# Moving the last wait of a ReLU-and-sum kernel from GpSimd to SyncE, and the semaphore clear to an earlier moment

## The chip, the cores and the metric

The kernel runs on one core of one Trainium2 chip. The metric is the device time of one execution in microseconds. Two numbers appear side by side throughout: the *time* of a run, and the *span* of the profile, which goes from the start of the program's first recorded instruction to the end of its last. The time is longer than the span (161.95 against 160.1 us in the first profile).

## The reference

```python
# x: (32, 512, 1024) float32
def reference(x):
    relu_x = np.maximum(x, 0)
    return np.sum(relu_x, axis=-1).astype(np.float32)   # (32, 512)
```

The kernel reads 67.11 MB and writes 0.07 MB.

## The kernel before

The 16384 rows are spread over 128 partitions, 128 rows each. SyncE issues all loads and all stores. ScalarE (ACT) clamps and VectorE (DVE) sums, or either one does both for a row. The last row of each partition comes in four pieces. Three stores write the sums out; the last one, 128 x 2 values, can only be issued when DVE has summed the last piece. A semaphore is used here as a counter that instructions raise and that other instructions wait for. Each load has one of its own, `act` and `dve` count finished instructions, and the three stores share `stored`.

What matters here is the end of the program. `relu_sum` ends with the third store, issued by SyncE:

```python
    # ... (relu_sum: loads, clamps, sums, two stores)
    nc.vector.tensor_scalar(                       # the last piece
        out=last[:, :], in0=last[:, :], scalar1=0.0, scalar2=None,
        op0=MAX, op1=ADD, accum_out=res[:, NT - 1 : NT],
    ).wait_op(sems.dve, before_last, "sem-ge").then_inc(sems.dve, 1)
    n_dve += 1
    store(NT - 2, 2, n_act, n_dve)                 # SyncE issues the last store
    return n_store
```

Then, in the closing block, GpSimd waits until all three stores have landed (16 increments each, 48 in the trace) and clears every semaphore of the kernel, with a drain and a range clear (one instruction for a range of semaphores: while it runs, from 159.93 to 160.06 us, the trace has one change of each of the kernel's 18, at 159.949 to 160.036) taken from the instructions that the framework had put there:

```python
    nc.cur_bb = nc.bb_map[tc.start_bb_name + "_end"]
    body = nc.cur_bb.bb.instructions
    clear = semaphore_clear(body)      # GpSimd: drain, range clear
    body.clear()
    nc.gpsimd.wait_ge(sems.stored, 16 * n_stores)
    body.extend(clear)
    # ...
```

GpSimd does nothing else in this kernel, apart from four memsets of 98 to 101 ns, a drain and three semaphore instructions, all over by 0.7 us.

## Time and profile before

| | before |
|---|---|
| time, median of the first 3 runs | 162.18 us (162.17 to 162.97) |
| profiled run: time / span | 161.95 / 160.1 us |
| DMA queue, share of 16 engines' span | 98.0% |
| DVE / ACT busy | 74% / 65% |
| last store, issue to landing | 1.4 us |

The first lines are from the page of the kernel before: the span, the busy times (engine, busy us, share, number of instructions) and the DMA queue (packets, MB, share).

```profile
span 160.1 us, 133 instructions
...
DVE 117.7 (74%) x43; ACT 104.2 (65%) x50; POOL 0.2 (0%) x4
...
q1 hardware_dynamic: 2592, 67.18, 98.0%
```

Its loads and stores keep the 16 DMA engines busy for 98.0% of the span, at 420 GB/s in the mean, so I take the kernel as bound by its loads almost from end to end. The change touches nothing of that, so the end has to be read closely. This is the instructions in order of time from 158.1 us on (start us, duration us, engine, line, operation):

```profile
157.92 0.43 DVE L205 TENSOR_SCALAR_CACHE_REDUCE piece<-piece 128x271 f32<-128x271 f32 x1
158.28 0.08 DVE L205 DVE_READ_ACCUMULATOR piece<-piece 128x1 f32 x1
158.39 0.33 SPq L105 DMA_DIRECT2D out_dram<-res  x1
```

That view leaves out drains and semaphore instructions, and so does the chain of waits, whose last line ends at 158.36 us:

```profile
157.92 0.44 DVE piece L205 x2
```

The chain says that the kernel's last work is DVE's. Yet the span lasts until 160.1. What fills the 1.7 us can be seen with the DMA issues (KB, us from issue to landing) and with the view of line 29 (`tc.close()`, where the framework made the instructions of the closing block; duration ns minimum/median/maximum, first and last start):

```profile
out_dram<-res SPq DMA_DIRECT2D x1, 1.0 KB, 1.4
```

```profile
engine op xcount: duration ns min/median/max, first and last start us, forms
L29 POOLq DRAIN  x1: 88/88/88, 159.8 to 159.8; - x1
L29 POOLq EVENT_SEMAPHORE_RANGE_CLEAR  x1: 136/136/136, 159.9 to 159.9; - x1
```

So the store takes 1.4 us, and GpSimd's drain and clear come after it. The trace splits the store's 1.39 us, from the start of the issue, into 0.82 us until its first packet starts (the issue itself lasts 0.33 us), 0.20 us of moving, and 0.37 us from the last packet's end to the last increment.

The views stop here, but the trace also records changes of semaphores, among them many that no instruction of the program names. Semaphore 2 is one of these. It moves in two groups at the end, and from 160.790 us on, ahead of the second group, 243 other semaphores change once each. I read the two groups as barriers, at which the engines wait for one another, and the changes between as a reset; the trace gives only the moments, so this is a reading. Read from the semaphore events, which no view of the profile prints (us from the span's start; the names of the engines are inferred, in the prediction and from the trace of the run s1_sync_clears below):

```
last increment of "stored" (the store has landed)   159.787
semaphore 2, first barrier:   1.003 PE   157.597 ACT   160.590 GpSimd   160.634 DVE   160.657 SyncE
                              then back  160.754  160.794  160.828  160.874
243 other semaphores change (the reset)             160.790 to 161.435
semaphore 2, second barrier                         161.704 to 162.061
```

By this reading each engine moves the semaphore once in the first barrier, one after the other: this is what *joining* the barrier means below. The four moves after the fifth are *the way back*. What follows the span, both barriers with the changes between them, is called the closing barriers below; the one that the engines join is the first.

The time of this run is 161.95 us, 0.11 us less than the last of these events.

### The profile page before, as it was taken

How to read it: one execution, taken by the hardware profiler on the slowest of the kernel's cores; microseconds unless marked ns; L12 is line 12 of the kernel's file. 1: busy time of each engine (PE TensorE's matmuls, PEld its weight loads, DVE VectorE, ACT ScalarE, POOL GpSimd, SP SyncE). 2: the span in 40 equal slices, each digit the busy share in tenths (PEclk: the TensorE clock that was granted, in tenths of full speed). 3: DMA queues.
4: the chain of work that ended last, by engine and by line, in shares of the span. 5: the costliest groups of instructions: out<-in, count | busy, mean ns of one | idle time of the engine just before them, and what ended most of it. 6: DMA issues, size and time to landing. Idle time of an engine off the chain costs nothing.

```text
span 160.1 us, 133 instructions
## 1 busy us (share of the span) xinstructions
DVE 117.7 (74%) x43; ACT 104.2 (65%) x50; POOL 0.2 (0%) x4
## 2 busy tenths in 40 slices
DVE  0000000009999499994999999999999999999994
ACT  3000059990799708995099942999239992599993
POOL 0000000000000000000000000000000000000000
DMA  7996996996996996997998999979969969999993
GB/s 262 524 524 262 524 524 262 524 524 262 524 508 278 524 508 278 524 475 311 524 409 377 524 393 393 524 328 459 524 278 508 524 262 524 393 393 422 409 400 96
DMA packets 2592, 67.18 MB, mean 420 GB/s; under 512 B 672, under 2 KB 1184, under 8 KB 1312
## 3 DMA queue, kind: packets, MB, share of 16 engines
q1 hardware_dynamic: 2592, 67.18, 98.0%
HBM read 67.11 MB, written 0.07 MB: 420 GB/s over the span
## 4 chain that ended last, share of the span: by engine, by line
DMA 43%; DVE 33%; ACT 17%; another core or an unknown queue 3%; SPq 1%; issue 0%
DVE res L120 32%; DMA io<-in_x_dram 25%; DMA piece<-in_x_dram 18%; ACT io L112 17%; SPq L94 1%; DVE piece L137 1%; DVE piece L205 0%
## 5 line engine op out<-in xcount | busy, mean ns | idle before, releaser
L120 DVE TENSOR_REDUCE res<-io 128x8 f32<-128x8192 f32 (+2 forms) x9 | 101.1, 11287 | 40.0 <-ACT io L112 40.0
L112 ACT ACTIVATE io<-io 128x8192 f32<-128x8192 f32 (+2 forms) x9 | 81.7, 9110 | 47.1 <-DMA io<-in_x_dram 47.1
L127 ACT ACTIVATE io<-io 128x1024 f32<-128x1024 f32 x20 | 20.9, 1043 | 5.4 <-DMA io<-in_x_dram 5.3
L137 DVE TENSOR_SCALAR_CACHE_REDUCE io<-io 128x1024 f32<-128x1024 f32 x13 | 15.0, 1214 | 0.2
L127 ACT ACTIVATION_READ_ACCUMULATOR io<-io 128x1 f32 x20 | 3.7, 187 | 0.0
L112 ACT ACT_TABLE_LOAD x1 | 1.3, 1283 | 0.8 <-PEq L259 0.8
L137 DVE TENSOR_SCALAR_CACHE_REDUCE piece<-piece 128x244 f32<-128x244 f32 (+2 forms) x3 | 1.2, 416 | 0.4 <-DMA piece<-in_x_dram 0.4
L137 DVE DVE_READ_ACCUMULATOR io<-io 128x1 f32 x13 | 1.1, 82 | 0.0
L205 DVE TENSOR_SCALAR_CACHE_REDUCE piece<-piece 128x271 f32<-128x271 f32 x1 | 0.4, 435 | 0.0
L137 DVE DVE_READ_ACCUMULATOR piece<-piece 128x1 f32 x3 | 0.3, 84 | 0.0
L259 POOL MEMSET const-bfloat16-1.0<- 128x1 bf16 x1 | 0.1, 101 | 0.0
L259 POOL MEMSET const-uint8-127<- 128x1 uint8 x1 | 0.1, 101 | 0.0
L259 POOL MEMSET const-float32-0.0<- 128x1 f32 x1 | 0.1, 98 | 0.2 <-issue 0.2
L259 POOL MEMSET const-float32-1.0<- 128x1 f32 x1 | 0.1, 98 | 0.0
L205 DVE DVE_READ_ACCUMULATOR piece<-piece 128x1 f32 x1 | 0.1, 82 | 0.0
## 6 DMA issues: line engine op xcount, KB each, us to landing
io<-in_x_dram SPq DMA_DIRECT2D x1, 4096.0 KB, 21.6
io<-in_x_dram SPq DMA_DIRECT2D x1, 2048.0 KB, 26.1
io<-in_x_dram SPq DMA_DIRECT2D x1, 1024.0 KB, 28.1
io<-in_x_dram SPq DMA_DIRECT2D x1, 512.0 KB, 28.9
piece<-in_x_dram SPq DMA_DIRECT2D x1, 134.0 KB, 28.5
piece<-in_x_dram SPq DMA_DIRECT2D x1, 130.0 KB, 28.6
piece<-in_x_dram SPq DMA_DIRECT2D x1, 126.0 KB, 28.7
piece<-in_x_dram SPq DMA_DIRECT2D x1, 122.0 KB, 28.8
```

What stands on the lines that cost most here:

```text
L94: dma = nc.sync.dma_start(out=dst, in_=src)
L112: i = nc.scalar.activation(out=ap, in_=ap, func=RELU)
L120: nc.vector.tensor_reduce(out=res[:, m : m + n], in_=ap, axis=mybir.AxisListType.X, op=ADD).wait_op(sems.act, n_act, "sem-ge").then_inc(se ...
L127: i = nc.scalar.activation(out=ap, in_=ap, func=RELU, accum_out=res[:, m : m + 1])
L137: i = nc.vector.tensor_scalar(out=ap, in0=ap, scalar1=0.0, scalar2=None, op0=MAX, op1=ADD, accum_out=accum_out,)
L205: nc.vector.tensor_scalar(out=last[:, :], in0=last[:, :], scalar1=0.0, scalar2=None, op0=MAX, op1=ADD, accum_out=res[:, NT - 1 : NT],).wai ...
L259: nc = _bacc.Bacc("TRN2", target_bir_lowering=False, num_devices=1)
```

## The change

The intent: GpSimd should not be the one to wait for the last store. SyncE waits for the stores and takes their semaphore down in the same instruction. GpSimd clears all other semaphores earlier, while the last store is under way; a new semaphore `issued`, raised by SyncE after the last issue, tells it when. The diff, without the removed helper `semaphore_clear`:

```diff
     nc.cur_bb = nc.bb_map[tc.start_bb_name + "_end"]
-    body = nc.cur_bb.bb.instructions
-    clear = semaphore_clear(body)
-    body.clear()
-    nc.gpsimd.wait_ge(sems.stored, 16 * n_stores)
-    body.extend(clear)
+    nc.cur_bb.bb.instructions.clear()
+    nc.sync.wait_ge(sems.stored, 16 * n_stores).then_inc(sems.stored, -16 * n_stores)
+    nums = sorted(s.num for s in (*sems.loads, sems.act, sems.dve, sems.issued))
+    cleared = range(nums[0], nums[-1] + 1)
+    assert len(cleared) == len(nums)
+    nc.gpsimd.wait_ge(sems.issued, 1)
+    nc.gpsimd.drain(semaphore_range=cleared)
+    nc.gpsimd.sem_clear(cleared)
...
         self.dve = tc.alloc_semaphore("dve")
+        self.issued = tc.alloc_semaphore("issued")
         self.stored = tc.alloc_semaphore("stored")
...
     store(NT - 2, 2, n_act, n_dve)
+    nc.sync.sem_inc(sems.issued, 1)
     return n_store
```

More of the change, by code (lines that the diff above doesn't have):

```diff
@@ L215, in relu_sum @@
     store(NT - 2, 2, n_act, n_dve)
+    nc.sync.sem_inc(sems.issued, 1)
     return n_store
-def semaphore_clear(instructions):
-    pool = [i for i in instructions if i.engine == mybir.EngineType.Pool]
-    at = next(
-        n for n, i in enumerate(pool) if getattr(i, "is_reset_sema", False)
-    )
-    return pool[at : at + 2]
 def issue_ahead_of_the_barrier(tc: tile.TileContext, n_loads: int):
```

## The prediction

> **What bounds the kernel now.** The busy line shows DMA near its limit almost everywhere (98.0% of the 16 engines' span, 420 GB/s mean); DVE is busy 74%, ACT 65%. The change touches none of that. It touches only what follows the last vector instruction, so I read that stage from the instructions in order of time and from the semaphore events of the trace:
>
> - 158.37 us: last DVE instruction ends. 158.39: SyncE issues the last store (0.33 us).
> - 159.79: the store's last semaphore increment arrives (1.4 us from issue to landing, DMA issues view).
> - 159.81: GpSimd's DRAIN passes its wait (88 ns); 159.93: the range clear (136 ns); it ends at 160.06, which ends the span of 160.1 us.
> - [...] semaphore 2 moves at 1.00, 157.60, 160.59, 160.63, 160.66 and then 160.75 to 160.87; [...] semaphore 2 moves again from 161.70 to 162.06.
>
> The moves at 1.00 and 157.60 follow the ends of PE's work and of ACT's (157.49, so 0.11 us later). DVE (done 158.37) and SyncE (done 158.73) left no own move before 160.59, so the engines join in a fixed order and the third one, which the others wait for, must be GpSimd. It joins 0.53 us after its clear ended. So the tail from landing to GpSimd's joining is 160.59 - 159.79 = 0.80 us, all on the critical path.
>
> **What the change does.** It adds one semaphore, one SyncE increment after the last store's issue, and one SyncE wait that also subtracts 48 (SyncE's semaphore instructions last 17 ns in this trace). It moves GpSimd's drain and clear to just after that increment: start about 158.76, end about 159.02, joining the barrier about 159.55 (my sums, from the same 0.25 and 0.53 us), some 0.24 us before the store lands. That work leaves the critical path. What stays is SyncE: wait passed at about 159.81, done 159.83, joining about 0.11 us later if it behaves as ACT did: 159.94 instead of the last join at 160.66. Estimated gain: 0.7 us[...]. The profile's span falls less, by 0.23 us to about 159.83, because 0.5 us of the gain lie after the last instruction.
>
> **Prediction: 161.50 us (range 161.25 to 161.95).** That is -0.4%. Chance of faster by over 2%: 0.01; within 2%: 0.98; slower by over 2%: 0.01.
>
> **What would show each step.** GpSimd's drain and clear start near 158.75 and end before 159.1, during the store. The last instruction is a SyncE semaphore instruction near 159.81. The third move of semaphore 2 comes near 159.55 and the last engine's join near 159.94; joining to end keeps its length (160.66 to 162.06, 1.40 us). Everything before 158.4 stays as it was; the store still takes 1.4 us.
>
> **What would make it wrong.** (1) The 0.53 us after GpSimd's clear may not be GpSimd's own: if any engine that leaves last pays it, SyncE pays it too and the gain is only about 0.25 us (161.9). (2) GpSimd's clear might take longer while transfers run, and join after SyncE. (3) One of three runs before took 162.97, 0.8 us above the others; noise in the loads of that size covers the gain. (4) The time may stop elsewhere than at the end of the closing barrier, so that less than all of the gain counts.

SyncE's join at 159.94 instead of 160.66 us is 0.72 us, put at 0.7 us, and the 162.18 us of before less 0.7 us is about 161.5 us. That a gain at the join reaches the end in full was an assumption of mine; in the traces the join comes 0.705 us earlier and the end 0.76 us.

## The result and the profile after

| | before | after |
|---|---|---|
| time, median of 6 runs | 162.13 us (161.98 to 162.97) | 161.31 us (161.06 to 161.45) |
| ratio | | 0.9941, 95% interval 0.9921 to 0.9961 |
| profiled run: time / span | 161.95 / 160.1 us | 161.37 / 160.0 us |
| last store, issue to landing | 1.4 us | 1.4 us |

Ratios are computed as the mean time of one kernel's fast runs over that of the other's of the same rounds, so they are not quite the ratio of the medians. In the later sets they are not quite the ratio of the plain means either; the gains given in us below are differences of plain means over all runs listed. Here the means are 162.24 and 161.29 us, a gain of 0.95 us, while the medians differ by 0.82 us. By the 2% mark the two kernels are the same; by the interval, the changed one is a little faster.

The same lines of the page of the changed kernel:

```profile
span 160.0 us, 135 instructions
...
DVE 117.7 (74%) x43; ACT 104.2 (65%) x50; POOL 0.2 (0%) x4
...
q1 hardware_dynamic: 2592, 67.18, 98.0%
```

Two instructions more, otherwise the same. The end in order of time, and the DMA issue of the last store:

```profile
158.11 0.43 DVE L209 TENSOR_SCALAR_CACHE_REDUCE piece<-piece 128x271 f32<-128x271 f32 x1
158.47 0.08 DVE L209 DVE_READ_ACCUMULATOR piece<-piece 128x1 f32 x1
158.58 0.33 SPq L109 DMA_DIRECT2D out_dram<-res  x1
```

```profile
out_dram<-res SPq DMA_DIRECT2D x1, 1.0 KB, 1.4
```

In this profiled run the last work came 0.19 us later than in the one of before, because the loads arrived later (the last increment for the third piece of the last row came at 157.429 us before and at 157.622 us here). Such shifts go both ways from run to run (the listed spans of before lie between 159.9 and 160.4 us); from here on the tail is therefore counted from the moment at which the store lands. The views of the lines that the change added (220: the increment; 45 and 46: drain and clear; 40: the last wait):

```profile
L220 SPq EVENT_SEMAPHORE  x1: 17/17/17, 159.0 to 159.0; - x1
...
L45 POOLq DRAIN  x1: 88/88/88, 159.0 to 159.0; - x1
...
L46 POOLq EVENT_SEMAPHORE_RANGE_CLEAR  x1: 136/136/136, 159.1 to 159.1; - x1
...
L40 SPq EVENT_SEMAPHORE  x1: 17/17/17, 160.0 to 160.0; - x1
```

The drain and the clear cost what they cost before, 88 and 136 ns, but they run at 159.0 and 159.1, ahead of the landing at 159.97. The SyncE wait is also to be seen among the waits of the DMA queue (engine and line, waited for, total us, times, longest us). It is put down to SyncE's own line, as the store that it waits for has no row of its own there:

```profile
SPq L40 <- SPq L40: 1.0, 1, 1.0
```

The semaphore events of both traces (the SyncE wait and GpSimd's drain and clear are instructions), in us after the store's landing:

```
                                           before    after
GpSimd: drain starts                       +0.024   -0.980
GpSimd: clear ends                         +0.277   -0.728
SyncE: last wait passes                       -     +0.017
semaphore 2: GpSimd joins                  +0.803   -0.201
             DVE joins                     +0.847   -0.157
             SyncE joins                   +0.870   +0.165
             next move (the way back)      +0.967   +0.210
             last move of first barrier    +1.087   +0.330
             last move of second barrier   +2.274   +1.513
```

The tail is 2.274 - 1.513 = 0.76 us shorter. Only 0.24 us of it lie inside the span (its end is 0.277 us after the landing before, 0.034 us after it now); 0.52 us lie after the span, in the closing barriers, which the page doesn't show. From the last move of the first barrier to the last of the second, both take 1.18 to 1.19 us.

### The profile page after: what moved, and what is told of

Same layout as the page of the kernel before. It is cut to its first block, busy times and chain, and to the rows that moved or that the text cites. A ratio compares the mean times of both kernels' runs of the same rounds, so it can differ in the third digit from the quotient of the medians.

```text
span 160.0 us, 135 instructions
## 1 busy us (share of the span) xinstructions
DVE 117.7 (74%) x43; ACT 104.2 (65%) x50; POOL 0.2 (0%) x4
## 4 chain that ended last, share of the span: by engine, by line
DMA 43%; DVE 33%; ACT 17%; another core or an unknown queue 3%; SPq 1%; issue 0%
DVE res L124 32%; DMA io<-in_x_dram 25%; DMA piece<-in_x_dram 18%; ACT io L116 17%; SPq L98 1%; DVE piece L141 1%; DVE piece L209 0%
```

## The experiments

Three sets, each on one chip with its own runs of the kernel before: first on chip 2, second on chip 1, third on chip 4. All gave correct results. Edits are shown against the changed kernel, unless said otherwise. The main question is where the 0.53 us between the end of GpSimd's clear and its joining come from, and whether the 0.95 us of the first rounds were all tail.

Two theories stood against each other for the first question: **G**, GpSimd needs this time to leave its program, whatever it did last; **C**, the range clear causes it, on any engine. For the second: **T**, only the tail changed; **R**, the work ahead of the last store became shorter as well.

### The kernel before against itself (n0_before_again)

No edit.

> The kernel before against itself, to see what five rounds can tell apart. Ratio 1.000, within 0.003 either way. In its trace the last store's landing to the last move of semaphore 2 takes 2.27 us, as in the first trace of before.

Measured: 162.04 us median against 161.91 us, ratio 1.0007 (0.9995 to 1.0020). Tail in the trace 2.276 us, against 2.274 in the first trace. Single runs range from 161.83 to 162.30, so differences of 0.2 us between two runs mean nothing, while the tail repeats within 0.003 us from trace to trace of one kernel (2.274 and 2.276 here, 1.513 to 1.516 in the changed kernel).

### The changed kernel again (a0_after_again, a1_after_third)

No edit.

> The changed kernel again. Theory T (only the tail after the landing changed): the landing to the last move of semaphore 2 takes 1.51 us, 0.76 us less than before, and the ratio is 0.9953; the 0.9941 of the first rounds was pulled down by one long run of before (162.97 us). Rival R (the change also shortens the work ahead of the store): the ratio is again 0.994 or less, and the store lands at least 0.15 us earlier after the span's start than in before, over several runs.

Measured: 161.26 against 161.91 us, ratio 0.9965 (0.9952 to 0.9979), a gain of 0.60 us in the mean; one of the five runs took 161.82, and the medians differ by 0.65 us. Tail 1.516 us. T's 0.9953 lies at the edge of the interval and R's 0.994 outside it. As that was no clear answer, it was run once more, on another chip:

> The changed kernel once more, on whatever chip this call gets. The tail in the traces is 0.76 us shorter than before, but the means of the first two comparisons differed by 0.95 and 0.60 us. If the difference is noise of the loads, this one falls between them, with the tail again at 1.51 us: ratio 0.9953, within 0.0015. If the first chip showed something of its own, this comes out near 0.9965 again.

Measured: 161.16 against 161.97 us, ratio 0.9949 (0.9936 to 0.9963), a gain of 0.82 us. Tail 1.514 us.

The three comparisons gave 0.95, 0.60 and 0.82 us, around the 0.76 us of the traces. R can be tested with the spans, since the span ends at a fixed distance after the landing (0.277 us before, 0.034 us after). Over the 32 runs of before whose spans are listed, the mean span is 160.12 us (spans are listed to 0.1 us), so the store lands at 159.84 on average; over the 16 runs of the changed kernel it is 159.93, so the store lands at 159.90. The changed kernel's stores land no earlier (0.06 us later, with runs scattering by 0.12 and 0.18 us, one standard deviation). R falls; T stands.

The number free of load noise is time less span: over the same runs it is 1.88 us before (1.84 to 1.93) and 1.35 us after (1.32 to 1.40). No run of one kernel overlaps with one of the other. That is the 0.5 us in the barrier; the other 0.24 us are the clear in the span.

### GpSimd waits last, but has nothing else to do then (g1_pool_last)

```diff
-    nc.sync.wait_ge(sems.stored, 16 * n_stores).then_inc(sems.stored, -16 * n_stores)
...
     nc.gpsimd.sem_clear(cleared)
+    nc.gpsimd.wait_ge(sems.stored, 16 * n_stores).then_inc(sems.stored, -16 * n_stores)
```

> GpSimd clears the others early, as in the changed kernel, but GpSimd itself, not SyncE, waits for the stores last and takes their semaphore down. Theory G (the 0.53 us that GpSimd takes to join the closing barrier belong to GpSimd, whatever it did last): it joins about 0.57 us after the landing, and the gain over before is about 0.24 us, ratio 0.9985. Theory C (the 0.53 us belong to the range clear): it joins about 0.15 us after the landing, two more hops follow, and the gain is about 0.70 us, ratio 0.9957.

Measured: 161.79 against 161.91 us, ratio 0.9991 (0.9977 to 1.0005). The view of its last wait:

```profile
L46 POOLq EVENT_SEMAPHORE  x1: 17/17/17, 159.8 to 159.8; - x1
```

Its last instruction is now a plain semaphore instruction of 17 ns, ending 0.041 us after the landing; it joins at 0.603 us, that is 0.56 us later. The tail is 2.071 us. G said 0.57 and C 0.15. The last instruction needn't be a clear for the delay: G stands for GpSimd. (GpSimd still cleared once, 0.76 us before its wait passed; a GpSimd that waits last and never clears was not run.) Most of the change's gain is gone, although the clear is as well hidden as in the changed kernel.

### SyncE does everything, GpSimd nothing (s1_sync_clears)

```diff
-    nc.sync.wait_ge(sems.stored, 16 * n_stores).then_inc(sems.stored, -16 * n_stores)
-    nums = sorted(s.num for s in (*sems.loads, sems.act, sems.dve, sems.issued))
+    nums = sorted(s.num for s in (*sems.loads, sems.act, sems.dve, sems.issued, sems.stored))
...
-    nc.gpsimd.wait_ge(sems.issued, 1)
-    nc.gpsimd.drain(semaphore_range=cleared)
-    nc.gpsimd.sem_clear(cleared)
+    nc.sync.wait_ge(sems.stored, 16 * n_stores)
+    nc.sync.drain(semaphore_range=cleared)
+    nc.sync.sem_clear(cleared)
...
-    nc.sync.sem_inc(sems.issued, 1)
```

> SyncE waits for the stores and then does the drain and the range clear of all semaphores itself; GpSimd has nothing to do at the end. Theory G: SyncE takes about 0.25 us for drain and clear and joins about 0.11 us after, 0.40 us after the landing; gain over before about 0.47 us, ratio 0.9971. Theory C: the 0.53 us go with the clear to SyncE; it joins about 0.80 us after the landing, gain under 0.12 us, ratio 0.9993 or more.

Measured: 161.42 against 161.91 us, ratio 0.9974 (0.9961 to 0.9987). The ratio is G's, but by two errors that cancelled. SyncE is quicker with the same two instructions than GpSimd: 7 ns for the drain, not 88, and for the clear 64 ns, not 136:

```profile
L44 SPq DRAIN  x1: 7/7/7, 159.9 to 159.9; - x1
...
L45 SPq EVENT_SEMAPHORE_RANGE_CLEAR  x1: 64/64/64, 159.9 to 159.9; - x1
```

The clear ends 0.133 us after the landing and SyncE joins at 0.244 us, 0.11 us later as G said and far from C's 0.80. The tail is 1.594 us, 0.68 us less than before, where I had expected 0.47. The time gained only 0.45 us in the mean, while the mean span was 160.2 us, with one run of 161.91: the last store landed late, by luck as far as five runs can tell. This trace also gives the order of the engines away: with GpSimd free, semaphore 2 moves at 157.673 (ACT), 157.711 (GpSimd), 158.579 (DVE, whose work ended at 158.434) and 160.099 (SyncE), each where that engine became free and not before its predecessor. A GpSimd that has had nothing to do joins 0.04 us after ACT.

### More work for GpSimd, to measure the slack (x2_more_clears, x8_more_clears)

```diff
-    nc.gpsimd.sem_clear(cleared)
+    for _ in range(3):          # 9 in the second kernel
+        nc.gpsimd.sem_clear(cleared)
```

> The changed kernel, with GpSimd's early range clear done three times instead of once. In the traces of the changed kernel GpSimd joins the closing barrier 0.20 us before the landing and SyncE 0.17 us after it; before, DVE's and SyncE's joins followed GpSimd's within 0.07 us. So I estimate a slack of about 0.30 us. Two more clears of 0.12 to 0.14 us move GpSimd's join by 0.24 to 0.28 us, to about 0.05 us after the landing. If GpSimd is off the critical path with that slack: SyncE's join and the last move stay at 0.17 and 1.51 us after the landing, ratio to before as the changed kernel's (0.9953). If GpSimd's work still counts: the last move comes 0.24 us or more later, ratio about 0.9968.

> The same with nine clears instead of one, eight more of 0.12 to 0.14 us: GpSimd would join 0.74 to 0.9 us after the landing and is on the critical path again. The last move of semaphore 2 comes 1.47 us after GpSimd's join (as before: 2.27 less 0.80), at 2.2 to 2.4 us after the landing; the whole gain is lost again, ratio to before 0.9996 to 1.0006. If it stays near 0.9953, GpSimd's join isn't what the closing barrier waits for and my reading of semaphore 2 is wrong.

Measured with three clears: 161.36 against 162.01 us, ratio 0.9958 (0.9946 to 0.9970). The clears last 132 to 136 ns but start every 0.16 us:

```profile
L47 POOLq EVENT_SEMAPHORE_RANGE_CLEAR  x3: 132/132/136, 159.0 to 159.4; - x3
```

So GpSimd joins at +0.110 us instead of the expected +0.05. The tail is 1.584 us, only 0.07 us longer than with one clear, though 0.31 us of work were added: the rest was slack. So neither outcome came true; the trace lies between them, and the ratio can't tell 0.9953 from 0.9968. As the last move comes 1.474 us after GpSimd's join (2.274 - 0.803 = 1.471 in the kernel before), GpSimd may join as late as +0.04 us before it counts, so the slack of the changed kernel is about 0.24 us, not the 0.30 that I had estimated.

Measured with nine: 162.25 against 162.01 us, ratio 1.0014 (1.0000 to 1.0027), one run of five at 162.89. (The plain means would give 1.0023; without that run they give 1.0015.)

```profile
L47 POOLq EVENT_SEMAPHORE_RANGE_CLEAR  x9: 132/132/136, 159.6 to 160.9; - x9
```

The last clear ends at +0.533 us, GpSimd joins at +1.061 (again 0.53 us later), and the tail is 2.534 us: the whole gain is lost and 0.26 us more, which is above the expected 2.2 to 2.4 us by the spacing of the clears; GpSimd's join and the ratio are above what was expected too. That the last move comes 1.02 us later than in the changed kernel (2.534 against 1.513 us), with GpSimd's join 1.26 us later, of which about 0.24 us were slack, shows that GpSimd's join is waited for, and supports the reading of semaphore 2.

### No clear at all (c0_no_clear)

```diff
-    nc.gpsimd.wait_ge(sems.issued, 1)
-    nc.gpsimd.drain(semaphore_range=cleared)
-    nc.gpsimd.sem_clear(cleared)
...
-    nc.sync.sem_inc(sems.issued, 1)
```

> The changed kernel without GpSimd's wait, drain and clear and without the semaphore that releases them; only SyncE's last wait with its subtraction is left. The other semaphores keep their counts[...]. If all of GpSimd's work was hidden: last move 1.51 us after the landing, ratio to before 0.9953, equal to the changed kernel. If the clear or SyncE's added increment cost something (for example by delaying the store's landing): issue to landing shorter than 1.39 us or last move earlier than 1.50 us.

Measured: 161.23 against 162.01 us, ratio 0.9955 (0.9943 to 0.9968). Issue to landing is 1.395 us (1.391 in the changed kernel), the tail 1.529 us (1.513). GpSimd's clear and SyncE's added increment cost nothing that the trace shows; hidden is hidden.

### ScalarE waits last (t1_scalar_last)

```diff
-    nc.sync.wait_ge(sems.stored, 16 * n_stores).then_inc(sems.stored, -16 * n_stores)
+    nc.scalar.wait_ge(sems.stored, 16 * n_stores).then_inc(sems.stored, -16 * n_stores)
```

> The changed kernel, with ScalarE instead of SyncE waiting for the stores last. ScalarE joins second, ahead of GpSimd, DVE and SyncE. If only GpSimd is slow to join: ScalarE joins about 0.15 us after the landing, three more hops of about 0.04 us follow, SyncE's join comes at 0.22 to 0.28 us, the last move at 1.6 us, about 0.1 us later than with SyncE, ratio to before 0.9958. If SyncE is special[...]: the last move at 2.0 us, ratio 0.9985.

Measured: 161.36 against 162.01 us, ratio 0.9963 (0.9951 to 0.9976). The wait is ACT's:

```profile
L40 ACTq EVENT_SEMAPHORE  x1: 17/17/17, 159.9 to 159.9; - x1
```

ACT joins at +0.183 us, 0.15 us after its wait ended; GpSimd, DVE and SyncE follow at +0.221, +0.264 and +0.288, and the way back starts at +0.385. The tail is 1.696 us, between before and after, 0.18 us longer than with SyncE where I had expected 0.1; had ACT needed GpSimd's 0.53 to 0.56 us, the rival outcome of 2.0 us would have come. So SyncE isn't special in being quick to join (ACT takes 0.15 us from the end of its wait, SyncE 0.13 us in the changed kernel); it has the best place of those measured, the last one in the order, so that no other engine has to follow.

### A drain for the last wait (d1_drain_waits)

```diff
-    nc.sync.wait_ge(sems.stored, 16 * n_stores).then_inc(sems.stored, -16 * n_stores)
+    nc.sync.wait_ge(sems.stored, 16 * n_stores)
+    nc.sync.drain()
...
-    nc.gpsimd.wait_ge(sems.issued, 1)
-    nc.gpsimd.drain(semaphore_range=cleared)
-    nc.gpsimd.sem_clear(cleared)
...
-    nc.sync.sem_inc(sems.issued, 1)
```

> A version meant to be a little better than the changed kernel: GpSimd has nothing to do at the end, and SyncE's last wait sits on a drain (7 ns in the trace where SyncE clears) instead of a semaphore instruction (17 ns); nothing is subtracted[...]. SyncE joins at about 0.02 + 0.01 + 0.11 = 0.14 us after the landing instead of 0.17, the last move at 1.48 us. In the time that is 0.03 us, too little to be told from the changed kernel: ratio to before 0.995. If the joining time doesn't depend on the instruction that waits: 0.17 and 1.51 us.

Measured: 161.19 against 161.97 us, ratio 0.9953 (0.9940 to 0.9965), beside the changed kernel's 161.16 us in the same rounds. SyncE joins at +0.145 us and the tail is 1.494 us, 0.02 us shorter than the changed kernel's, close to the 1.48 us hoped for; the time cannot show it. The kernel without a clear is the nearer comparison, as GpSimd is idle in both: against it the tail is 0.035 us shorter. It also leaves all counts of the kernel's semaphores in place at the end of the program; its runs gave correct results all the same. No version beats the changed kernel by anything measurable.

The tails together, from the landing of the last store, with the means of the runs beside them:

| kernel | last engine to finish | GpSimd joins | SyncE joins | tail | tail against before | mean time against before |
|---|---|---|---|---|---|---|
| before | GpSimd, clear | +0.803 | +0.870 | 2.274 | | |
| nine clears | GpSimd, clear | +1.061 | +1.127 | 2.534 | +0.26 | +0.37 |
| GpSimd waits last | GpSimd, wait | +0.603 | +0.670 | 2.071 | -0.20 | -0.19 |
| ScalarE waits last | ACT, wait | +0.221 | +0.288 | 1.696 | -0.58 | -0.58 |
| SyncE clears | SyncE, clear | early | +0.244 | 1.594 | -0.68 | -0.45 |
| three clears | GpSimd joins just late | +0.110 | +0.177 | 1.584 | -0.69 | -0.66 |
| no clear | SyncE, wait | early | +0.175 | 1.529 | -0.75 | -0.71 |
| changed kernel | SyncE, wait | -0.201 | +0.165 | 1.513 | -0.76 | -0.95, -0.60, -0.82 |
| drain waits | SyncE, drain | early | +0.145 | 1.494 | -0.78 | -0.75 |

"Early" means ahead of the last store's issue. The times follow the tails within 0.16 us, except in two comparisons that one long run pulled: the first of the changed kernel (0.19 us off, where a run of before took 162.97) and SyncE clears (0.23 us off). Without its run of 162.89 the nine clears' mean is 0.24 us above before, beside the 0.26 us of the tail.

## Why the prediction was right or wrong

**What bounds the kernel, and what the change touches: right.** The DMA queue is 98.0% busy before and after, and nothing ahead of the store changed that the runs can tell. Over the runs whose spans are listed the store lands at 159.84 us before and 159.90 us after.

**The tail as the only place of the gain: right.** GpSimd's drain and clear moved into the store's flight; the last instruction is SyncE's, 17 ns long, 0.017 us after the landing; GpSimd joins 0.20 us before the landing (I had said 0.24); SyncE joins at +0.165 us (I had said 0.15); the span falls by 0.24 us relative to the landing (I had said 0.23), and the larger part of the gain lies outside the span.

**The doubt about the 0.53 us: settled as the prediction had it.** They belong to GpSimd. It needs 0.53 to 0.56 us from its last instruction to joining, after a clear as after a plain wait, and whether a store is in flight or not (0.53 us before, with the changed kernel and with nine clears, 0.56 us in g1_pool_last); SyncE needs 0.11 to 0.14 us and ACT 0.11 to 0.15 us. What GpSimd does in this time is open: it executes no instruction of the program then, and no run here looks inside.

**The sum: too small by 0.06 us.** I predicted 0.7 us, and the traces show 0.76 us. SyncE's join came 0.705 us earlier (0.870 to 0.165), as foreseen. The term that failed is the stretch from SyncE's join to the last move, which I took as the same in both kernels ("joining to end keeps its length (160.66 to 162.06, 1.40 us)"). It shrank from 1.404 to 1.348 us. In all six traces in which DVE joins just ahead of SyncE, the way back starts 0.12 us after DVE's join (0.967 - 0.847 before, 0.385 - 0.264 with ScalarE waiting), and SyncE's join falls inside that gap. In the other six, the changed kernel's among them, DVE had joined long before, and the next move follows SyncE's join after 0.043 to 0.045 us instead of 0.097 us. What DVE does in these 0.12 us no trace shows.

**The range: wrong on the fast side.** Measured as a ratio, the first rounds gave 0.9941, which on the 162.18 us of before is 161.22 us, just below my lower bound of 161.25 us (the median of the six runs themselves, 161.31 us, lies inside the range). Beside the 0.06 us above, the step that failed is the treatment of noise. I wrote that "noise in the loads of that size covers the gain", as if it could only hide it. In fact the run of 162.97 us was in the mean of before: without it that mean is 162.09 instead of 162.24 us, and the gain 0.81 instead of 0.95 us. So, of the 0.25 us by which the mean gain exceeded my 0.7 us, 0.15 us are this one run, 0.06 us the stretch after SyncE's join, and the remaining 0.04 us are within the scatter of the loads. The two later comparisons, at 0.60 and 0.82 us, lie on both sides of the 0.76 us of the traces, which supports that reading. The run of 162.97 us left no trace, but one late run did, the 162.89 us of the nine clears, and there the delay lies ahead of the tail. Of the 16 increments of the last load's semaphore 15 had come at 157.77 us and the last one at 158.50 us, 0.86 us after the last packet of the loads had ended (0.22 to 0.27 us in the four traces compared: the kernel before and the changed one, two each). DVE waited 0.64 us for it, the figure in brackets:

```profile
158.61 0.43 DVE L210 TENSOR_SCALAR_CACHE_REDUCE piece<-piece 128x271 f32<-128x271 f32 x1 [0.64 <-DMA piece<-in_x_dram]
```

What held that increment back is open, and whether the run of 162.97 us was late for the same reason is not shown.

Left open on purpose: a kernel that doesn't wait for the last store at all. It was not tried, and no run here shows whether its output would be complete at the end.

## What to carry to other kernels

As far as this one kernel shows, the end of a kernel's span is not the end of its time (160.1 against 161.95 us): an engine that still has to join the closing barrier counts, and a slow joiner, here GpSimd with 0.53 to 0.56 us, should get its last instruction early. Give the wait for the last store to an engine that joins quickly and last in the order, here SyncE with 0.11 to 0.14 us, and let housekeeping such as clears (88 and 136 ns on GpSimd) run while the store is in flight (1.39 us). For gains of half a microsecond, compare tails from a fixed event of the trace, such as the landing of the last store, since a single late run moved the mean here by 0.15 us.
